# Two modulation parts as matmuls of 32 columns between the product terms, weights split on one engine, wider parts and earlier token norms

## The chip, the cores and the metric

The kernel runs on one core of a Trainium2 chip. TensorE is called PE here, VectorE DVE, ScalarE ACT, GpSimd POOL, SyncE SP (it issues DMAs). The metric is the time of one execution in device microseconds (us); the lower the better. PE's clock has two levels here, 1.2 and 2.4 GHz, and the profile gives the granted share of the upper one.

## The reference, cut to what matters

One transformer block for 1024 tokens of width 1024, all in float32. The change lies in the first part only: the modulation vectors, the first norm, and the combined input projection (1024 x 1280) whose columns are Fourier channels (512), queries (512), keys (128) and values (128).

```
ada = silu(c) @ w_ada + b_ada                  # c: 1 x 1024, w_ada: 1024 x 6144
sh1, sc1, g1, sh2, sc2, g2 = split(ada, 6)     # six parts of 1024
h = rmsnorm(x, norm_mix_g) * (1 + sc1) + sh1   # 1024 tokens x 1024
uqkv = h @ w_in                                # 1024 x 1280
...                                            # Fourier mix, windowed attention, w_out
x = x + g1 * mixed
h = rmsnorm(x, norm_ffn_g) * (1 + sc2) + sh2
...                                            # expert-choice MoE, 16 experts
return x + g2 * moe
```

## The kernel before, in words

A float32 product is made of three matmuls: each operand is split in a rounded high part and the rest (`split`, lines 76 to 78: ACT writes hi, another engine lo = src - hi), and hi x hi, lo x hi and hi x lo are summed in PSUM. `wh`/`wl` are the halves of a weight chunk of `w_in` (128 rows x 1280), `hh`/`hl` those of the transposed, normed and modulated tokens `hf`.

Three phases: modulation and input projection, up to about 183 us; Fourier mix, attention, output projection and router, up to 459 us; then the 16 experts.

In the first phase the tokens stand in 8 tiles (t) of 128, the width in 8 chunks (k) of 128. **The pair**: tiles 0 and 1 are multiplied together, chunk by chunk, while the 8 chunks of `w_in` and the columns of parts 1 (sc1) and 0 (sh1) of `w_ada` still arrive. For each k or pair of ks, `load_mod` brings columns of both parts (128 x 8 x 256, or halves of 128 x 4 x 512), `mod_mac` multiplies them on DVE with silu(c) and sums over j (L111 for the first, L113 for the rest), `mod_sum` sums over the partitions with matmuls against `ones` (L209), and `mod_cols` makes the columns G1c and sh1c from that (L216 to L218). `chunk` transposes (L226), applies G1c and sh1c on ACT (L233, hf) and splits into hh (ACT, L77) and hl (POOL, L78). `take` splits the weights: wh on ACT (L349), then `low_w` makes wl (L277), the first `WLO[k]` columns on POOL and the others on DVE. `project` (L332) issues a unit: for each of hh x wh, hl x wh, hh x wl and each tile, three matmuls of 512, 512 and 256 columns into three PSUM accumulators (names pu, pu, pv, or px for the second tile of the pair).

**Tiles 2 to 7** follow, each in two chunks of four units (m = 0 to 11, the steps of `seq`): m = 0, 1 are tile 2, m = 2, 3 tile 3, and so on. The last kv accumulator of each tile stands in one PSUM buffer (pv, one buffer), which `finish` empties on ACT (L338 un, L340 kk, L341 vf) and DVE (L339). Beside them run, in steps after each unit (`bg_tick`): `qknorm` for each tile done (squares on ACT, sums on DVE L245, then on POOL a power L248, and the products L252, L254 and L257 into kd; two transposes on PE, L264, and the split of their result into khi and klo), and `ada_row` for the four other parts of `w_ada`, in 8 rows of 512 columns (DVE macs L111 and L113, one matmul with `ones` on PE, L142, an add on DVE, L143, and a store). The norm of the next tile but one's tokens is `norm_x`: ACT squares with a sum (L152), DVE, POOL's power (xr, L155), ACT's scaling of the tokens in place (L186).

Up to the last product of the pair the order on each engine is the order of the code (`in_order`). Behind that a scheduler sets the order of each engine when the program is built. Each engine runs its instructions strictly in that order, so that an instruction that waits holds up all behind it.

Of the kernel before, what the change touches and what calls it, by code (L numbers as in the profile page):

```python
# [11 lines left out]
F32 = mybir.dt.float32  # L12
# [9 lines left out]
NT = 8  # L22
# [10 lines left out]
SCRATCH = 4096  # L33
WLO = (0, 768, 768, 1280, 768, 1280, 768, 768)
SB, PB, WB, YB = 9, 2, 4, 3
# [8 lines left out]
def block_kernel(ctx: ExitStack, tc: tile.TileContext, t_in, out):  # L44
# [35 lines left out]
    def raw(shape):  # L80
        return raw1.tile(shape, F32, name="raw", tag="raw")
# [3 lines left out]
    c_t = cst.tile([128, 8], F32, name="c_t")  # L85
    c_act = cst.tile([128, 8], F32, name="c_act")
    cols = cst.tile([128, 4, 8], F32, name="cols")
# [42 lines left out]

    def ada_row(acc, br, px, part, cc):
        col = part * 1024 + cc * 512
        for jh in range(2):
            u = raw([128, 4, 512])
            SP.dma_start(u, w_ada_v[:, jh * 4:jh * 4 + 4, col:col + 512])
            for j in (0, 2):
                mac(acc, u[:, j:j + 2], 2, jh * 4 + j)
                yield
        SP.dma_start(br, b_ada[:, col:col + 512])
        yield  # L140
        p = px()
        PE.matmul(p[0:1], ones[:, 0:1], acc, start=True, stop=True)  # L142
        DVE.tensor_tensor(br, p[0:1], br, op=OP.add)  # L143
        SP.dma_start(md[part - 2:part - 1, cc * 512:cc * 512 + 512], br)

# [65 lines left out]

# [8 lines left out]
    def chunk(ts, kc0, nk):  # L220
# [59 lines left out]
    mods, maccs, msums = {}, {}, {}  # L280
    load_mod(0)
# [40 lines left out]
    def ada_all():  # L322
        for part in (2, 4, 3, 5):
            for cc in range(2):
                yield from ada_row(racc, br[0:1], px, part, cc)

    def project(ts, kc, hs_, o):
        for l, r in ((0, w_h), (1, w_h), (0, w_l)):
            for s_ in range(len(ts)):
                lhs = hs_[l][:, o + s_ * 128:o + s_ * 128 + 128]  # L330
                for acc, c0, c1 in zip(accs[s_], (0, 512, 1024), (512, 1024, 1280)):
                    PE.matmul(acc[:, :c1 - c0], lhs, r[kc][:, c0:c1], start=(kc == 0 and l == 0 and r is w_h),  # L332
                              stop=(kc == 7 and r is w_l))

    def finish(s_, t):
        au, aq, ak = accs[s_]
        kk = ust.tile([128, 128], F32, name="kk", bufs=2)
        ACT.activation(u_n[t], au, AF.Copy)  # L338
        DVE.tensor_copy(qn[t], aq)  # L339
        ACT.activation(kk, ak[:, :128], AF.Copy)  # L340
        ACT.activation(vf[:, t, :], ak[:, 128:256], AF.Copy)  # L341
        bg.append(qknorm(t, kk))

    pair = (0, 1)
    accs = [[pu(), pu(), (pv, px)[s_]()] for s_ in pair]

    def take(k):
        r = wraw.pop(k)
        ACT.activation(w_h[k], r, AF.Copy)  # L349
        if WLO[k] == 1280:  # L350
            low_w(k, r)
            h = chunk(pair, k, 1)
        else:
            h = chunk(pair, k, 1)
            low_w(k, r)
# [23 lines left out]
    take(2)
    column(4)  # L380
    take(3)
    column(5)
    project(pair, 2, hs.pop(2), 0)
    scales(4, 5)
    take(4)
    load_x(2)
    column(6)
    project(pair, 3, hs.pop(3), 0)
    take(5)
    column(7)  # L390
    load_x(3)
    project(pair, 4, hs.pop(4), 0)
    project(pair, 5, hs.pop(5), 0)
    scales(6, 7)
    take(6)
# [38 lines left out]
    for m, (t, kc0) in enumerate(seq):  # L434
        hs_ = nxt
        if m == len(seq) - 1:
# [4 lines left out]
            for n, wid in ((4, 512), (2, 256), (1, 128), (1, 128)):  # L441
                basis(n, wid)
        if kc0 == 0:
            if t + 2 < NT:
                load_x(t + 2)
            if t + 1 < NT:
                norm_x(t + 1)
            accs = [[pu(), pu(), pv()]]
        if m + 1 < len(seq):
            nxt = chunk((seq[m + 1][0],), seq[m + 1][1], 4)  # L450
        for a in range(4):
            project((t,), kc0 + a, hs_, a * 128)
            if m == 0 and a == 1:
                DVE.scalar_tensor_tensor(gg, qg, HD ** -0.5, kg, op0=OP.mult, op1=OP.mult)
# [891 lines left out]
```

## Time and profile before

| | us |
|---|---|
| runs of the kernel before | 1076.07, 1079.47, 1079.58 (median 1079.47) |
| the profiled execution | 1078.71, its span 1076.90, mean granted PE clock 0.949 |
| start to the first product of the pair | 0 to 16.12 |
| the pair, k = 0 to 7 | 16.12 to 70.50 |
| m = 0, 1 | 70.50 to 87.72 |
| m = 2 | 87.72 to 105.91 |
| m = 3 to 9 | 105.91 to 168.97 |
| m = 10, 11 | 168.97 to 183.20 |
| Fourier mix, attention, output projection, router | 183.20 to 459.00 |
| 16 experts | 459.00 to 1076.90 |

The bounds of the stages are the starts of matmuls of line L332 in the timeline of PE (70.50 is the first matmul of m = 0, and so on). Each row of a timeline is a run of like instructions: start, time from the first start to the last end, engine, line, operation, output and inputs, partitions x elements, count, and in square brackets the idle time ahead of it and who ended it. A float32 matmul leaves two records. A matmul's record ends later than the next may start, so that what one costs is read from start to start.

### The profile page before, as it was taken

How to read it: one execution, taken by the hardware profiler on the slowest of the kernel's cores; microseconds unless marked ns; L12 is line 12 of the kernel's file. 1: busy time of each engine (PE TensorE's matmuls, PEld its weight loads, DVE VectorE, ACT ScalarE, POOL GpSimd, SP SyncE). 2: the span in 40 equal slices, each digit the busy share in tenths (PEclk: the TensorE clock that was granted, in tenths of full speed). 3: DMA queues.
4: the chain of work that ended last, by engine and by line, in shares of the span. 5: the costliest groups of instructions: out<-in, count | busy, mean ns of one | idle time of the engine just before them, and what ended most of it. 6: DMA issues, size and time to landing. Idle time of an engine off the chain costs nothing.

```text
span 1076.9 us, 13229 instructions
## 1 busy us (share of the span) xinstructions
PE 969.0 (90%) x4681; PEld 756.4 (70%) x4681; DVE 845.9 (79%) x1223; ACT 636.9 (59%) x846; POOL 540.3 (50%) x345
## 2 busy tenths in 40 slices
PE   4797999979999996496769999999999999999996
PEld 3675767747777675374658777877787778777885
DVE  6845884687666959689688898889888988898894
ACT  3353434576455442264437777777777777777782
POOL 2646465132433334355472875587558755772203
PEclk9798999979999999598889999999999999999998
DMA  9765674262312136895689999999999999999922
GB/s 318 246 210 212 220 266 150 82 195 61 111 70 89 65 132 215 326 321 192 229 260 339 410 372 374 369 411 370 373 369 411 371 371 371 411 371 358 376 110 40
DMA packets 95499, 283.97 MB, mean 264 GB/s; under 512 B 7892, under 2 KB 25480, under 8 KB 95304
## 3 DMA queue, kind: packets, MB, share of 16 engines
q1 hardware_dynamic: 90824, 266.34, 66.7%
q0 software_dynamic: 4608, 16.78, 6.1%
q8 instruction: 37, 0.61, 0.2%
q14 instruction: 30, 0.25, 0.1%
HBM read 263.79 MB, written 21.40 MB: 265 GB/s over the span
## 4 chain that ended last, share of the span: by engine, by line
PE 64%; DVE 15%; issue 6%; ACT 4%; DMA 2%; POOL 2%; POOLq 0%; DVEq 0%; ACTq 0%; SPq 0%
PE pa L72 13%; PE pa L73 13%; PE pa L74 13%; PE pu L332 4%; PE pt L1192 2%; ACT wh L77 2%; PE pt L640 2%; PE yp L653 2%; DVE sc L805 2%; DVE wl L78 2%; PE pj L74 2%; PE pj L72 2%; PE pj L73 2%; DVE sc L806 2%; DVE ws L113 2%
## 5 line engine op out<-in xcount | busy, mean ns | idle before, releaser
L78 DVE TENSOR_TENSOR wl<-raw,wh 128x2048 fp32r<-128x2048 f32 (+1 forms) x183 | 418.1, 2309 | 63.5 <-ACT wh L77 62.6
L77 ACT ACTIVATE wh<-raw 128x2048 fp32r<-128x2048 f32 (+2 forms) x209 | 367.8, 1780 | 85.0 <-PE pa L73 81.3
L1165 POOL TENSOR_SCALAR oneh<-tri_f,pos 128x128 bf16<-128x128 f32 x102 | 189.5, 1871 | 4.1 <-PE pa L1047 3.3
L73 PE MATMUL pa<-wh,t1l 128*128 128x512 f32 x384 | 151.8, 395 | 7.8 <-DVE t1l L78 7.8
L72 PE MATMUL pa<-wh,t0h 128*128 128x512 f32 x384 | 155.8, 406 | 0.0
L73 PE MATMUL pa<-wh,t0l 128*128 128x512 f32 x384 | 153.4, 400 | 0.0
L72 PE MATMUL pa<-wh,t1h 128*128 128x512 f32 x384 | 153.1, 399 | 0.0
L74 PE MATMUL pa<-wl,t0h 128*128 128x512 f32 x384 | 152.6, 397 | 0.0
L74 PE MATMUL pa<-wl,t1h 128*128 128x512 f32 x384 | 151.3, 394 | 0.0
L1207 POOL TENSOR_TENSOR ys<-ys,g_r 128x512 f32<-128x512 f32 x30 | 53.5, 1803 | 124.7 <-ACT ys L1206 124.7
L73 PEld LDWEIGHTS pa<-wh,t1l 128*128 128x128 f32 x384 | 72.6, 189 | 24.0 <-DVE t1l L78 8.3
L74 PEld LDWEIGHTS pa<-wl,t0h 128*128 128x128 f32 x384 | 73.6, 192 | 17.0
L72 PEld LDWEIGHTS pa<-wh,t0h 128*128 128x128 f32 x384 | 73.6, 192 | 16.2 <-ACT t0h L77 0.2
L73 PEld LDWEIGHTS pa<-wh,t0l 128*128 128x128 f32 x384 | 73.6, 192 | 16.1 <-DVE t0l L78 0.4
L74 PEld LDWEIGHTS pa<-wl,t1h 128*128 128x128 f32 x384 | 72.6, 189 | 17.0 <-DVE wl L78 0.4
L72 PEld LDWEIGHTS pa<-wh,t1h 128*128 128x128 f32 x384 | 72.4, 189 | 15.9
L1182 POOL DMA_INDIRECT xe<-h2d,idx x16 | 16.9, 1055 | 115.7 <-DVE gt L1179 110.7
L78 POOL TENSOR_TENSOR wl<-raw,wh 128x1024 fp32r<-128x1024 f32 (+1 forms) x26 | 56.7, 2208 | 22.3 <-ACT wh L77 22.2
L78 POOL TENSOR_TENSOR hl<-hf,hh 128x512 fp32r<-128x512 f32 (+1 forms) x20 | 25.5, 1274 | 62.9 <-ACT hh L77 43.6
L1210 POOL DMA_INDIRECT out_dram<-ys,idx x16 | 50.9, 3183 | 10.6 <-DVE ys L1209 6.4
L611 DVE CUSTOM_DVE_ANT_0 sb<-lg,bias,sink 128x384 f32<-128x384 f32 (+1 forms) x64 | 35.0, 579 | 26.7 <-PE lg L609 15.7
L233 ACT ACTIVATE hf<-pt,sh1c,G1c 128x128 f32<-128x128 f32 (+1 forms) x56 | 22.6, 479 | 53.3 <-PE pt L226 36.2
(310 smaller groups left out, 1809.5 us busy)
## 6 DMA issues: line engine op xcount, KB each, us to landing
raw<-in_w_gate_dram SPq DMA_DIRECT2D x64, 1024.0 KB
raw<-in_w_up_dram SPq DMA_DIRECT2D x64, 1024.0 KB
raw<-in_w_down_dram SPq DMA_DIRECT2D x63, 1024.0 KB
raw<-in_w_ada_dram SPq DMA_DIRECT2D x16, 1024.0 KB
raw<-in_w_ada_dram SPq DMA_DIRECT2D x16, 512.0 KB
xt<-in_x_dram SPq DMA_DIRECT2D x8, 512.0 KB
raw<-in_w_out_dram SPq DMA_DIRECT2D x4, 1024.0 KB
raw<-in_x_dram SPq DMA_DIRECT2D x8, 512.0 KB
```

The lines of the kernel that those rows point to most:

```text
L72: PE.matmul(o, lh, rh, start=start, stop=False)
L73: PE.matmul(o, ll, rh, start=False, stop=False)
L74: return PE.matmul(o, lh, rl, start=False, stop=stop)
L77: ACT.activation(hi, src, AF.Copy)
L78: return (eng or DVE).tensor_tensor(lo, src, hi.bitcast(F32), op=OP.subtract)
L113: DVE.scalar_tensor_tensor(acc, u[:, j, :], w, acc, op0=OP.mult, op1=OP.add)
L233: ACT.activation(hf[:, a * w:a * w + w], tp[:, a * w:a * w + w], AF.Identity, scale=G1c[:, kc:kc + 1], bias=sh1c[:, kc:kc + 1])
L332: PE.matmul(acc[:, :c1 - c0], lhs, r[kc][:, c0:c1], start=(kc == 0 and l == 0 and r is w_h), stop=(kc == 7 and r is w_l))
L611: DVE.tensor_tensor_reduce(sb[:, :wid], lg[:, :wid], bias[:, kv * 4 + i, j0:j0 + wid], 1.0, sk[:, i:i + 1], op0=OP.add, op1=OP.max, accum_ ...
L1165: (POOL if t < shared else DVE).tensor_scalar(oneh[:, t, :], slots, pos[:, t, e:e + 1], None, op0=OP.is_equal)
L1207: POOL.tensor_tensor(ys[:, cs_], ys[:, cs_], g2_r[:, cs_], op=OP.mult)
L1210: POOL.indirect_dma_start(out=out2, out_offset=bass.IndirectOffsetOnAxis(ap=idx[:, :1], axis=0), in_=ys, in_offset=None, compute_op=OP.add)
```

## The change

- `c_act` becomes 128 x 8 x 32, zero but for its first column. `part_row` multiplies it (32 columns as stationary operand) with the raw columns of `w_ada`, on PE; term j goes to the PSUM partitions 32g to 32g + 31 with g = j mod 4, in one bank (px). This takes the place of `mod_mac` on DVE. `mod_sum` copies that bank to SBUF on ACT and sums it with `ones`.
- `terms` is `project` as a generator; the part rows stand in PE's order between its second term (hl x wh) and its third (hh x wl).
- wl and hl are made on DVE alone, 1280 and up to 512 wide. POOL has neither.
- In the pair `pair_chunk` (hf, hh, hl) stands ahead of `weights` (wh, wl). Four loads of modulation columns and three of weights are issued at once.
- The pair's two key and value accumulators share one bank (pv). Tiles 2 to 7 alternate between px and pv. The transposes of kd go to pt from the start.
- The four other parts of `w_ada` are made 1024 wide: raws of 128 x 2 x 1024, two to three fetched ahead, 8 macs for a part, two matmuls (32 columns, two column groups) and one add of 64 x 512.
- Token tiles are loaded three ahead and normed two ahead; tiles 2 and 3 are both normed ahead of the pair's last two products. `finish` does the query copy, kk and vf ahead of un.

The core of the diff:

```diff
-WLO = (0, 768, 768, 1280, 768, 1280, 768, 768)
+    def part_row(p, g, j, u, start, stop):
+        PE.matmul(p[32 * g:32 * g + 32, :u.shape[-1]], c_act[:, j, :], u, start=start, stop=stop)
...
     def mod_mac(h):
-        ks, j, n = halves[h]
-        if j == 0:
-            maccs[ks] = qn[4 + (0, 1, 2, 0, 3, 0, 0)[ks[0]]][:, :len(ks) * 256]
-        mac(maccs[ks], mods.pop(h), n, j)
+        ks, j0, n = halves[h]
+        if j0 == 0:
+            msums[ks] = px()
+        u = mods.pop(h)
+        for j in range(n):
+            part_row(msums[ks], (j0 + j) % 4, j0 + j, u[:, j], j0 + j < 4, j0 + j >= 4)
     def mod_sum(*ks):
-        acc = maccs.pop(ks)
-        mp = pt()
+        mp = msums[ks]
+        acc = qn[4 + (0, 1, 2, 0, 3, 0, 0)[ks[0]]][:, :len(ks) * 256]
+        ACT.activation(acc, mp[:, :len(ks) * 256], AF.Copy)
...
-        split(hi[:, :n], lo[:, :n], hf[:, :n], POOL)
+        split(hi[:, :n], lo[:, :n], hf[:, :n])
...
-    px_ = [px]
+    px_ = [pt]
...
     def low_w(kc, r):
-        c = WLO[kc]
-        for eng, c0, c1 in ((POOL, 0, c), (DVE, c, 1280)):
-            if c0 < c1:
-                eng.tensor_tensor(w_l[kc][:, c0:c1], r[:, c0:c1], w_h[kc][:, c0:c1].bitcast(F32), op=OP.subtract)
+        after["w"] = DVE.tensor_tensor(w_l[kc], r, w_h[kc].bitcast(F32), op=OP.subtract)
...
+    def ada_parts(acc, br, parts):
...
+        fetch()
+        fetch()
+        for part in parts:
+            for q in range(4):
+                fetch()
+                u = us.pop(0)
+                for j in range(2):
+                    yield
+                    mac(acc, u[:, j:j + 1], 1, 2 * q + j)
...
+            p = pt()
+            for g in range(2):
+                PE.matmul(p[32 * g:32 * g + 32], ones[:, 0:32], acc[:, 512 * g:512 * g + 512], start=True, stop=True)
+            yield
+            DVE.tensor_tensor(br, p[:64], br, op=OP.add)
...
+    def pair_products(k, n):
+        p = terms(pair, k, hs.pop(k), 0)
+        next(p)
+        next(p)
+        if n < 8:
+            column(n)
+            column(n + 1)
+        drain(p)
+        if n < 8:
+            scales(n, n + 1)
+        p = terms(pair, k + 1, hs.pop(k + 1), 0)
+        next(p)
+        if n < 8:
+            pair_chunk(n)
+            weights(n)
+        next(p)
+        if n < 8:
+            pair_chunk(n + 1)
+        drain(p)
+        if n < 8:
+            weights(n + 1)
...
-                load_x(t + 2)
-            if t + 1 < NT:
-                norm_x(t + 1)
-            accs = [[pu(), pu(), pv()]]
+                load_x(t + 3)
+            if t + 2 < NT:
+                norm_x(t + 2)
+            accs = [[pu(), pu(), (px, pv)[t % 2]()]]
```

In ACT's order around k = 1 and k = 2 (wh with its number is the high half of one weight chunk; hh is that of the tokens' chunk), before:

```order
L349 ACTIVATE wh_154<-ws 128x1280
L233 ACTIVATE hf<-pt,sh1c,G1c 128x256
L77 ACTIVATE hh<-hf 128x256
L349 ACTIVATE wh_156<-u_hi 128x1280
L233 ACTIVATE hf<-pt,sh1c,G1c 128x256
L77 ACTIVATE hh<-hf 128x256
```

and after:

```order
L241 ACTIVATE qn_117<-px 128x256
L266 ACTIVATE hf<-pt,sh1c,G1c 128x256
L76 ACTIVATE hh<-hf 128x256
L384 ACTIVATE wh_159<-ws 128x1280
L241 ACTIVATE qn_118<-px 128x512
L266 ACTIVATE hf<-pt,sh1c,G1c 128x256
L76 ACTIVATE hh<-hf 128x256
L384 ACTIVATE wh_161<-u_hi 128x1280
```

The copy of the part rows came in, and wh of a chunk moved from ahead of that chunk's hh to behind it.

In PE's order around the start of m = 2 (the first rows are its first unit or units), before:

```order
L332 MATMUL pu<-wh_152,hh 128x512 x2
L332 MATMUL pv<-wh_152,hh 128x256
L332 MATMUL pu<-wh_152,hl 128x512 x2
L332 MATMUL pv<-wh_152,hl 128x256
L332 MATMUL pu<-wl_153,hh 128x512 x2
L332 MATMUL pv<-wl_153,hh 128x256
L332 MATMUL pu<-wh_154,hh 128x512 x2
L332 MATMUL pv<-wh_154,hh 128x256
L332 MATMUL pu<-wh_154,hl 128x512 x2
L264 MATMUL px<-ident,kd 128x128 x2
L332 MATMUL pv<-wh_154,hl 128x256
```

and after:

```order
L259 MATMUL pt<-ident,xt 128x128 x4
L362 MATMUL pu<-wh_157,hh 128x512 x2
L362 MATMUL pv<-wh_157,hh 128x256
L362 MATMUL pu<-wh_157,hl 128x512 x2
L362 MATMUL pv<-wh_157,hl 128x256
L362 MATMUL pu<-wl_158,hh 128x512 x2
L362 MATMUL pv<-wl_158,hh 128x256
L297 MATMUL pt<-ident,kd 128x128 x4
```

Both pairs of transposes of kd (tiles 0 and 1) now stand together behind the first unit, on the two buffers of pt; before they stood in the second and the third unit, on px. The second pair takes the buffer of pt that the chunk of m = 3 (the L259 ahead of the unit) fills and that ACT's hf of that chunk (L266) empties.

In ACT's order over the same place, after (L217 is the scaling of a token tile that `norm_x` ends with, here of tile 5; the last hf is that of m = 3's chunk):

```order
L276 ACTIVATE ws<-qn_109 128x512
L266 ACTIVATE hf<-pt,sh1c,G1c 128x128 x4
L183 ACTIVATE junk,xs<-xt 128x1024
L76 ACTIVATE hh<-hf 128x512
L217 ACTIVATE xt<-xt,xr 128x1024
L375 ACTIVATE un_122<-pu 128x512
L373 ACTIVATE kk<-px 128x128
L374 ACTIVATE vf<-px 128x128
L275 ACTIVATE ws<-kk 128x128
L266 ACTIVATE hf<-pt,sh1c,G1c 128x128 x4
```

The scaling stands ahead of tile 2's `finish` and of the hf of m = 3, as its counterpart L186 (there of tile 4) did before.

And in POOL's order, after, up to that tile's xr (the last row):

```order
L186 TENSOR_TENSOR xr<-xs,mhalf 128x1 x3
L281 TENSOR_TENSOR qr<-qs,mhalf 128x10
L285 TENSOR_TENSOR qn_108<-qn_108,qr 128x512
L287 TENSOR_TENSOR kk<-kk,qr 128x128
L290 TENSOR_TENSOR kd<-kk,gg 128x2x64 x2
L281 TENSOR_TENSOR qr<-qs,mhalf 128x10
L285 TENSOR_TENSOR qn_109<-qn_109,qr 128x512
L287 TENSOR_TENSOR kk<-kk,qr 128x128
L290 TENSOR_TENSOR kd<-kk,gg 128x2x64 x2
L186 TENSOR_TENSOR xr<-xs,mhalf 128x1
```

The two splits hl that stood ahead of and behind this chain are gone; the chain of both tiles still stands ahead of xr.

## Rows read from the trace of the kernel before

**Rows 1.** The page's chain of the work that ended last, by engine, as shares of the span.

```profile
PE 64%; DVE 15%; issue 6%; ACT 4%; DMA 2%; POOL 2%; POOLq 0%; DVEq 0%; ACTq 0%; SPq 0%
```

**Rows 2.** The windows of the stages: start and end, length, busy time (and count) of PE, PE's weight loads, DVE, ACT and POOL, PE's granted clock, share of the DMA engines, GB/s.

```profile
16.12:70.50 54.38, 43.49 (x195) 35.10 (x195) 39.16 (x54) 20.78 (x34) 26.48 (x18) 0.87 0.71 239
70.50:87.72 17.22, 17.22 (x86) 12.84 (x85) 11.44 (x19) 8.57 (x22) 12.02 (x9) 1.00 0.94 334
87.72:105.91 18.19, 11.91 (x49) 8.80 (x48) 8.90 (x14) 5.36 (x13) 11.11 (x12) 0.81 0.52 177
105.91:168.97 63.06, 60.56 (x303) 45.44 (x302) 48.70 (x71) 27.91 (x65) 31.44 (x26) 1.00 0.66 234
168.97:183.20 14.23, 14.23 (x76) 12.00 (x75) 5.37 (x9) 3.47 (x12) 10.82 (x11) 1.00 0.37 115
183.20:459.00 275.80, 240.99 (x1289) 175.28 (x1288) 198.71 (x616) 139.40 (x373) 94.75 (x88) 0.91 0.40 136
459.00:1076.90 617.90, 578.40 (x2690) 465.46 (x2690) 526.47 (x430) 425.39 (x323) 351.14 (x175) 0.97 0.89 329
```

**Rows 3.** The timeline of PE in the pair: the first matmuls of the products k = 0, 1, 2, 3, 4 and 6, and the sum of the modulation columns 4 and 5.

```profile
16.12 1.22 PE L332 MATMUL pu<-wh,hh 128*128 128x512 f32 x2 [1.16 <-ACT hh L77]
...
24.68 0.73 PE L332 MATMUL pu<-wh,hh 128*128 128x512 f32 x2 [1.54 <-ACT hh L77]
...
32.41 0.74 PE L332 MATMUL pu<-wh,hh 128*128 128x512 f32 x2 [0.63 <-ACT hh L77]
...
42.58 1.83 PE L209 MATMUL pt<-ones,qn 128*128 128x2 f32 x8 [5.24 <-DVE qn L113]
...
44.59 1.20 PE L332 MATMUL pu<-wh,hh 128*128 128x512 f32 x2
...
50.44 0.70 PE L332 MATMUL pu<-wh,hh 128*128 128x512 f32 x2
...
60.12 0.73 PE L332 MATMUL pu<-wh,hh 128*128 128x512 f32 x2 [0.63 <-ACT hh L77]
```

**Rows 4.** Windows of two stretches behind a long idle time of PE (columns as in rows 2).

```profile
44.59:50.44 5.85, 5.85 (x23) 4.89 (x21) 5.67 (x9) 2.14 (x3) 4.27 (x3) 0.60 0.00 0
94.71:99.80 5.09, 5.09 (x16) 4.21 (x17) 0.82 (x1) 2.58 (x7) 1.30 (x1) 0.50 0.79 294
```

**Rows 5.** The timeline of PE at one of the ada rows (L142, one float32 matmul of 512 columns, two records) with the transpose behind it, and in the attention, where two float32 matmuls of 256 columns go to two halves of the array, 64 columns each (L653, four records), with the transposes behind them.

```profile
150.01 1.02 PE L142 MATMUL px<-ws,ones 128*1 128x512 f32 x2
150.96 0.33 PE L226 MATMUL pt<-ident,xt 128*128 128x128 f32 x1
...
394.69 0.65 PE L653 MATMUL yp<-pT,vf 128*64 128x256 f32 x4
395.27 0.66 PE L752 MATMUL pt<-ident,raw 128*128 128x128 f32 x4
```

**Rows 6.** The same view of PE for a stretch of 20 ns at one of those pairs: the records that began in it.

```profile
391.72 0.44 PE L653 MATMUL yp<-pT,vf 128*64 128x256 f32 x2 [0.48 <-DVE ss L724]
```

**Rows 7.** The timeline of ACT: one weight split in the pair, between two splits of the tokens.

```profile
24.53 1.28 ACT L349 ACTIVATE wh<-u_hi 128x1280 fp32r<-128x1280 f32 x1
```

**Rows 8.** The timeline of DVE: a weight chunk's low half done whole, the macs of the modulation columns 4 and 5 in the pair, and a mac of 1024 columns in the second phase.

```profile
14.67 1.48 DVE L277 TENSOR_TENSOR wl<-ws,wh 128x1280 fp32r<-128x1280 f32 x1
...
32.26 10.17 DVE L113 SCALAR_TENSOR_TENSOR qn<-raw,c_act,qn 128x512 f32<-128x512 f32 x7
...
241.76 1.21 DVE L872 SCALAR_TENSOR_TENSOR G_r<-G_r,raw 128x1024 f32<-128x1024 f32 x1
```

**Rows 9.** The timeline of PE in m = 0 and 1: the bias table's matmul and one ada row.

```profile
74.19 1.02 PE L456 MATMUL pt<-ws,rb 32*8 32x512 f32 x2
...
84.58 1.02 PE L142 MATMUL px<-ws,ones 128*1 128x512 f32 x2
```

**Rows 10.** The timeline of PE at the start of m = 2.

```profile
87.72 0.71 PE L332 MATMUL pu<-wh,hh 128*128 128x512 f32 x2
94.71 0.58 PE L332 MATMUL pv<-wh,hh 128*128 128x256 f32 x1 [6.28 <-ACT vf L341]
```

**Rows 11.** The timeline of ACT at that place: the scaling of tile 4's tokens, and the hf of the chunk behind it.

```profile
92.70 1.15 ACT L186 ACTIVATE xt<-xt,xr 128x1024 f32<-128x1024 f32 x1 [10.17 <-POOL xr L155]
...
94.74 1.51 ACT L233 ACTIVATE hf<-pt,sh1c,G1c 128x128 f32<-128x128 f32 x4
```

**Rows 12.** The timeline of POOL ahead of that: the first step of tile 0's key and query norms, the split hl that follows tile 1's last step, and tile 4's xr.

```profile
77.27 2.45 POOL L248 TENSOR_TENSOR qr<-qs,mhalf 128x10 f32<-128x10 f32 x1 [1.18 <-DVE qs L246]
...
89.97 1.73 POOL L78 TENSOR_TENSOR hl<-hf,hh 128x512 fp32r<-128x512 f32 x1
91.66 1.00 POOL L155 TENSOR_TENSOR xr<-xs,mhalf 128x1 f32<-128x1 f32 x1
```

**Rows 13.** The groups of instructions by line and shape in m = 3 to 9, of PE and of DVE: busy time, mean ns of one, idle time ahead of them and what ended it.

```profile
L142 PE MATMUL px<-ws,ones 128*1 128x512 f32 x12 | 6.1, 590 | 2.2 <-DVE ws L113 2.1
...
L113 DVE SCALAR_TENSOR_TENSOR ws<-raw,c_act,ws 128x512 f32<-128x512 f32 x42 | 36.5, 868 | 0.9
```

**Rows 14.** The waits of PE from 16 to 70.5 us: engine, tile and line, what it waited for, us in total, times, longest.

```profile
PE pt L209 <- DVE qn L113: 5.2, 1, 5.2
PE pu L332 <- ACT hh L77: 3.9, 4, 1.5
...
PE pu L332 <- POOL wl L277: 0.8, 1, 0.8
```

More of the change, by code (lines that the diff above doesn't have):

```diff
@@ L85, in block_kernel @@
     c_t = cst.tile([128, 8], F32, name="c_t")
-    c_act = cst.tile([128, 8], F32, name="c_act")
+    c_act = cst.tile([128, 8, 32], F32, name="c_act")
     cols = cst.tile([128, 4, 8], F32, name="cols")
@@ L97, in block_kernel @@
     SP.dma_start(c_t, t_in["c"].rearrange("b (p j) -> (b p) j", j=8))
-    ACT.activation(c_act, c_t, AF.Silu)
+    POOL.memset(c_act, 0.0)
+    ACT.activation(c_act[:, :, 0], c_t, AF.Silu)
     POOL.memset(ones, 1.0)
@@ L129, in drain, with fetch, store @@
             pass
[L131 to L144, printed above, removed]
+    def ada_parts(acc, br, parts):
+        todo = [(part, q) for part in parts for q in range(4)]
+        us, rows_ = [], []
+        def fetch():
+            if todo:
+                part, q = todo.pop(0)
+                us.append(raw([128, 2, 1024]))
+                SP.dma_start(us[-1], w_ada_v[:, 2 * q:2 * q + 2, part * 1024:part * 1024 + 1024])
+        def store():
+            if rows_:
+                part = rows_.pop()
+                for g in range(2):
+                    SP.dma_start(md[part - 2:part - 1, g * 512:g * 512 + 512], br[32 * g:32 * g + 1])
+        fetch()
[7 more added lines that the diff above has]
+                    mac(acc, u[:, j:j + 1], 1, 2 * q + j)
+                if q == 0:
+                    store()
+                if q == 1:
+                    for g in range(2):
+                        c0 = part * 1024 + 512 * g
+                        SP.dma_start(br[32 * g:32 * g + 1], b_ada[:, c0:c0 + 512])
+            yield
+            p = pt()
+            for g in range(2):
+                PE.matmul(p[32 * g:32 * g + 32], ones[:, 0:32], acc[:, 512 * g:512 * g + 512], start=True, stop=True)
+            yield
+            DVE.tensor_tensor(br, p[:64], br, op=OP.add)
+            rows_.append(part)
+        store()
     w_ada_v = w_ada.rearrange("(p j) c -> p j c", j=8)
@@ L292, in block_kernel @@
     load_mod(2)
+    load_mod(3)
+    wraw[2] = load_w(2)
     rb = p1.tile([32, 8], F32, name="rb")
@@ L322, in ada_all, with terms @@
     def ada_all():
[L323 to L327, printed above, removed]
+        yield from ada_parts(racc, br, (2, 4, 3, 5))
+    def terms(ts, kc, hs_, o):
         for l, r in ((0, w_h), (1, w_h), (0, w_l)):
@@ L331, in project @@
                 for acc, c0, c1 in zip(accs[s_], (0, 512, 1024), (512, 1024, 1280)):
-                    PE.matmul(acc[:, :c1 - c0], lhs, r[kc][:, c0:c1], start=(kc == 0 and l == 0 and r is w_h),
-                              stop=(kc == 7 and r is w_l))
+                    first = kc == 0 and l == 0 and r is w_h and not (s_ and c0 == 1024)
+                    PE.matmul(acc[:, :c1 - c0], lhs, r[kc][:, c0:c1], start=first, stop=(kc == 7 and r is w_l),
+                              skip_group_check=c0 == 1024)
+            yield
+    def project(ts, kc, hs_, o):
+        drain(terms(ts, kc, hs_, o))
     def finish(s_, t):
@@ L341, in finish, with weights @@
         ACT.activation(vf[:, t, :], ak[:, 128:256], AF.Copy)
+        ACT.activation(u_n[t], au, AF.Copy)
         bg.append(qknorm(t, kk))
     pair = (0, 1)
-    accs = [[pu(), pu(), (pv, px)[s_]()] for s_ in pair]
-    def take(k):
+    both_kv = pv()
+    accs = [[pu(), pu(), both_kv[:, 256 * s_:256 * s_ + 256]] for s_ in pair]
+    def weights(k):
         r = wraw.pop(k)
         ACT.activation(w_h[k], r, AF.Copy)
[L350 to L355, printed above, removed]
+        low_w(k, r)
         if k + 3 < 8:
             wraw[k + 3] = load_w(k + 3)
-        hs[k] = h
     def column(h):
         mod_mac(h)
-        if h + 3 < 8:
-            load_mod(h + 3)
+        if h + 4 < 8:
+            load_mod(h + 4)
     def scales(*ks):
@@ L367, in scales, with pair_chunk @@
         mod_cols(*ks)
-    hs = {}
-    take(0)
-    column(1)
-    project(pair, 0, hs.pop(0), 0)
+    def pair_chunk(k):
+        hs[k] = chunk(pair, k, 1)
+    def pair_products(k, n):
[19 more added lines that the diff above has]
+            weights(n + 1)
+    hs = {}
+    weights(0)
+    load_mod(4)
+    pair_chunk(0)
+    p = terms(pair, 0, hs.pop(0), 0)
+    next(p)
+    next(p)
+    column(1)
+    drain(p)
+    scales(1)
+    pair_chunk(1)
+    weights(1)
+    p = terms(pair, 1, hs.pop(1), 0)
+    next(p)
+    next(p)
     column(2)
-    scales(1)
-    take(1)
     column(3)
-    project(pair, 1, hs.pop(1), 0)
+    drain(p)
     scales(2, 3)
[L379 to L385, printed above, removed]
+    pair_chunk(2)
+    weights(2)
+    pair_chunk(3)
+    weights(3)
+    pair_products(2, 4)
     load_x(2)
[L387 to L390, printed above, removed]
     load_x(3)
[L392 to L395, printed above, removed]
+    pair_products(4, 6)
     norm_x(2)
-    take(7)
+    norm_x(3)
     project(pair, 6, hs.pop(6), 0)
@@ L402, in block_kernel @@
     ws = [stage(), stage()]
-    sq, racc = ws[0][:, :640], ws[0][:, 640:1152]
-    br = ws[1][:, :512]
+    sq, br = ws[0][:, :640], ws[0][:64, 640:1152]
+    racc = ws[1][:, :1024]
+    POOL.memset(br, 0.0)
     for s_ in pair:
@@ L453, in block_kernel @@
             if m == 0 and a == 1:
-                DVE.scalar_tensor_tensor(gg, qg, HD ** -0.5, kg, op0=OP.mult, op1=OP.mult)
+                with tc.issue_after(after["w"].ins):
+                    DVE.scalar_tensor_tensor(gg, qg, HD ** -0.5, kg, op0=OP.mult, op1=OP.mult)
                 p = pt()
@@ L891, in block_kernel @@
     ydone, x2s, x2Ts, xts, ylive = {}, {}, {}, {}, [0]
-    after = {}
     fr, qks, ready, sp = {}, {}, [], [None]
```

14 lines of the change are left out of this document (6 added, 8 removed).

## The prediction

> **What bounds the kernel now.** I read the chain of the work that ended last first: PE holds 64% of it [rows 1]. Then the windows by stage [rows 2]: the change touches only what ends at 183.20 us, and there PE is either busy or waited for in every stretch. In m = 0, 1 and in m = 10, 11 it is busy all the time (17.22 of 17.22, 14.23 of 14.23), in m = 3 to 9 for 60.56 of 63.06. So what counts is PE's own work, and its waits, which the page's waits put in two places. In the pair (54.38 us, 43.49 of them busy) it waits 5.2 us for DVE's macs, four times for hh, 3.9 us in all, and 0.8 for POOL's share of wl [rows 14]. In m = 2 it waits 6.28 us for ACT's vf [rows 10]. Both long waits cost twice: behind the first the granted clock is 0.60 over 5.85 us, behind the second 0.50 (the lower level, 1.2 GHz) over 5.09 [rows 4]. The second and third phases, 275.80 and 617.90 us, begin with work that needs the last tile's projection, and their code is unchanged; I let them shift as a block, by what 183.20 shifts.
>
> A unit of the projection takes 14.23 / 8 = 1.78 us at the full clock, the transposes with it [rows 2], a product of the pair (two tiles) 3.5, two of its three terms 2.4, or 4.7 at the lower level.
>
> **The cost of a part row.** No row of before has a stationary operand of 32 columns in four column groups. A float32 matmul of 512 columns alone takes 0.95 us from start to next start (150.01 to 150.96) [rows 5]. Two in two column groups do run together: both began within 20 ns [rows 6], and the two of 256 columns took 0.58 (394.69 to 395.27) [rows 5] where one alone would take half of 0.95, 0.48. So the bounds for four of 512 are 0.95 (all at once) and 3.8 (one after another). I take 0.95, nearest to the row with two groups, whose surplus over one is only 0.10. Eight rows of 512 then are 1.9 us, the 256 wide set 1.0, or 1.6 at the lower level.
>
> The Trainium skill speaks against full packing: "TensorE: Matmul & The Clock Gate", section "Measured speedup vs the span model", gives 2.38 times for three column tiles of 32 and N = 512, 3.07 times for four row tiles. By that four would take 4 x 0.95 / 3.07 = 1.24 us, an estimate, and the sum below would be 2 us worse; no run here shows it yet.
>
> **The pair, stretch by stretch** (the times of before are the differences of their starts [rows 3]). The first product starts at 16.2 (16.12): the part rows of set 0 replace 8 macs, but ACT's squares of the tokens still hold its copy.
> - k = 0 to 1, before 8.56: plus 1.6 for part rows at the lower level, plus 1.27 because wh of k = 1 now stands behind hh in ACT's order (a split takes 1.28 [rows 7]) and PE needs both, minus 0.6, since the third term then runs at the full level. 10.85, so 27.05.
> - k = 1 to 2, before 7.73: plus 1.9 and 1.27 likewise. 10.9, so 37.95.
> - k = 2 to 3, before 12.18, with the wait for DVE of 5.24. That wait goes, since DVE has no macs, and POOL's 0.8 goes too. What remains is two terms 3.75 (I let half of it fall in the lower level), part rows 1.9, third term 1.2, sum 0.8. 7.65, so 45.6. The copy on ACT, as long as un's, lies beside the third term.
> - k = 3 to 4, before 5.85 at 0.60 of the clock: without the idle time ahead of it 4.25, so 49.85.
> - k = 4 to 6, before 9.68: plus 1.9 part rows and 0.8 for the sum and its transposes, minus 1.9 for the wait for the chunk, which now lies beside k = 5. 10.5, so 60.35.
> - k = 6 to m = 0, before 10.38: plus 1.0 as the bias table's matmul (1.02, 74.19 [rows 9]) now stands ahead of m = 0; the two token norms ahead of the products hold the transposes of tile 2 for about as long as before. 11.15, so 71.5.
>
> The pair: +1.0 us. The gain from the wait is spent on part rows (7.3 in all) and on wh. DVE's wl (1.48 for a chunk alone [rows 8]) lies beside the first two terms; if it should not, 0.3 to 1 us at each of the seven.
>
> **m = 0, 1.** The bias matmul (1.0, moved) and an ada row (0.95, 84.58 [rows 9]) go, with their gaps 2.5 us. 17.22 to 14.75, so m = 2 starts at 86.2 (87.72).
>
> **m = 2: the wait changes its place.** Before, PE waited for pv, emptied by ACT behind the scaling at 92.70, which waited 10.17 us for POOL's xr [rows 11]; that stood behind the norms of tiles 0 and 1, from 77.27 to 89.97, and a split of 1.73 [rows 12]. With px and pv in turn this wait goes. But both pairs of transposes of kd now stand behind the first unit of m = 2, and the second pair needs the buffer that hf of m = 3 frees; that hf stands on ACT behind a scaling (tile 5) that needs an xr behind the same chain on POOL. The sums of tile 0 come later: on DVE ahead of them stand the bias add and five macs of 1024 (1.21 each [rows 8]); I get 80.05 for the chain's start. 80.05 + 12.7 (as 77.27 to 89.97) = 92.75, xr 1.0 = 93.75, from the scaling to the end of hf 3.6 (92.70 to 96.25 [rows 11]) = 97.4. PE reaches the place at 88.1 and waits 9.2 us, then loses some 2.5 at the lower level, as in rows 4. Behind it are 3 units, the transposes of kd and an ada sum: m = 3 starts at 107.0 (105.91). 20.8 for 18.19, +2.6. Queued behind the waiting transposes is all of PE's work; ACT's khi and DVE's klo of tiles 0 and 1 come late, and nobody needs them before the attention.
>
> **m = 3 to 9.** Seven chunks of 4 units at 7.37 are 51.6. Before, six ada rows (12 records, 6.1 busy), 2.1 us of waits for their macs [rows 13], the kd transposes and small gaps make the rest of 63.06. After, three pairs of ada sums, each pair in two column groups at 1.0, and 1.4 of kd transposes: 55.9, so -7.1. DVE bears it: 42 macs of 868 ns [rows 13] become about half as many of 1.21 plus contention, and the splits hl come to it, 0.7 each; POOL, which split weights beside DVE's macs in the pair, where they took 10.17 / 7 = 1.45 each [rows 8], loses its splits. m = 10, 11 stay at 14.2.
>
> **The sum.** +1.0 - 2.5 + 2.6 - 7.1 = -6.0. I add 1.5 for small waits for DVE (in m = 1 to 8 it is busy some nine tenths of PE's time, and hl now queues behind macs of 1.21): -4.5. Against the profiled execution that is 1078.71 - 4.5 = 1074.2; the median stands 0.76 above it, so I say 1074.5. Unknown sizes: the wait in m = 2 (7 to 12 us, so +-2.5), the clock in the pair (+-2), DVE (0 to 4): the likeliest case's own range is 1069.5 to 1079.
>
> **The rivals.**
> - Part rows packed less well. If four groups give only what two give in rows 5, 0.95 / 0.58 = 1.64 of 2, that is 3.3 of 4: 1.15 for 0.95, +0.2 for each of 7 sets; if they go in pairs, +0.95 for each, 6.5 us: 1076 to 1081. For it: no row shows four. Against: the 20 ns.
> - **Slower: the part rows go one after another.** Each half of a set then costs 3.8 in place of 0.95, six halves +17, the narrow set +3, on PE's path since the third term waits behind them: +20, partly made up by waits that shrink, so 1088 to 1094. It decides from 1.6 us for a half: there -4.5 is used up. For it: all four write one bank. Against: the two groups of rows 6 do so too.
> - The wait in m = 2 does not come: POOL's chain without its splits, and the ada loads that no longer hold DVE, let xr come before 90. 1065 to 1070. For it: two splits leave POOL. Against: the chain's start hangs on DVE, with longer macs.
> - DVE becomes the bound of tiles 2 to 6: if the macs of 1024 cost twice 868 ns, a tile has 8 of 1.74 plus 4.3 of other work, 18.2 us for a PE time of 16; -7.1 falls to about 0, 1081.
>
> **How the numbers follow.** As forecast 0.55, packed less 0.20, one after another 0.08, no wait in m = 2 0.08, DVE the bound 0.09. A measurement of this kernel tells about 0.5% (5.4 us) from no change. Faster by more: half of the first case (0.28), a fifth of the second and the whole fourth, 0.40. Slower by more: the third, a tail of the second and the last, 0.15. Within: 0.45. The range leaves out most of the third case and the end of the fourth: 1067 to 1084.
>
> **What would show it.** In the profile after: the four L117 of a half start together and the half takes about 1 us; PE's third product starts without a wait for DVE; wh, not hh, ends the waits at k = 1 and 2; an idle time of 7 to 12 us ahead of the second pair of L297 at 88 us, ended by POOL's kd or ACT's hf, with 0.5 of the clock behind it; m = 3 to 9 at 56 us with little waiting for DVE. I am wrong if a half takes over 1.6 us, if that wait is missing, or if hl on DVE ends waits of PE in every chunk.

## The result, and the profile after

The changed kernel took 1072.54 us (median of 5 runs, 1069.07 to 1073.78), before 1079.47: the ratio is 0.9932, with a 95% interval of 0.9910 to 0.9955. Its profiled execution took 1073.78, with a span of 1071.9 and a mean granted clock of 0.952.

The stages, from the same starts of matmuls (of L362 now):

| stage | before | forecast | after |
|---|---|---|---|
| first product of the pair | 16.12 | 16.2 | 16.93 |
| the pair | 54.38 | 55.3 | 54.57 |
| m = 0, 1 | 17.22 | 14.75 | 15.05 |
| m = 2 | 18.19 | 20.8 | 18.95 |
| m = 3 to 9 | 63.06 | 55.9 | 56.52 |
| m = 10, 11 | 14.23 | 14.2 | 14.38 |

The windows of after, with the columns of [rows 2]:

```profile
16.93:71.50 54.57, 47.91 (x261) 34.16 (x261) 16.80 (x34) 23.71 (x39) 1.63 (x3) 0.94 0.88 300
71.50:86.55 15.05, 15.05 (x82) 12.77 (x81) 14.15 (x18) 9.69 (x24) 6.96 (x5) 1.00 0.83 286
86.55:105.50 18.95, 11.48 (x51) 8.38 (x50) 6.67 (x11) 5.15 (x13) 11.84 (x13) 0.73 0.36 139
105.50:162.02 56.52, 56.52 (x303) 45.64 (x302) 40.80 (x48) 26.21 (x62) 23.65 (x17) 1.00 0.64 233
```

In the pair DVE's busy time fell from 39.16 to 16.80 and POOL's from 26.48 to 1.63, and PE's rose from 43.49 to 47.91: the work moved, and the stage took the same time. From m = 3 to 9 PE is busy all the time, and most of the gain lies there (6.54 us; m = 0, 1 gives 2.17, and the other stages lose a little). At the first matmul of the second phase after is ahead by 184.36 - 177.41 = 6.95 us. The profiled execution gives 2 us of it back further on: its second phase took 276.66 us up to the first product of the experts, before 273.72, and what follows took 1 us less. In the kernels below, with the same code there, the second phase took 272.6 to 274.6; why it was longer in this execution isn't shown. So the two profiled executions are 4.93 apart, the medians 6.93.

The timeline of PE in the pair of after (L117 are the part rows, two records each; L259 the transposes of tile 2), against [rows 3]:

```profile
21.49 1.60 PE L117 MATMUL px<-raw,c_act 128*32 128x256 f32 x16
...
27.64 0.74 PE L362 MATMUL pu<-wh,hh 128*128 128x512 f32 x2 [2.57 <-ACT wh L384]
...
30.18 1.92 PE L117 MATMUL px<-raw,c_act 128*32 128x512 f32 x16
...
37.12 1.22 PE L362 MATMUL pu<-wh,hh 128*128 128x512 f32 x2 [2.36 <-ACT wh L384]
...
41.68 2.60 PE L117 MATMUL px<-raw,c_act 128*32 128x512 f32 x16
...
46.28 0.72 PE L362 MATMUL pu<-wh,hh 128*128 128x512 f32 x2
...
66.03 0.66 PE L259 MATMUL pt<-ident,xt 128*128 128x128 f32 x4 [1.73 <-ACT xt L217]
```

A set of eight rows of 512 takes 1.92 at the full clock; at 30.18 three of its records began within 20 ns and a fourth within 120 ns, so the four groups do run together. The wait of 5.24 for DVE is gone, and wh, no longer hh, ends the waits at k = 1 and 2. Behind the second of them the products run at the lower level (the record of 1.22 for two matmuls, 0.72 at the upper one).

And at m = 2 of after, on PE, with the granted clock behind this wait and behind that at k = 2 in two windows, against [rows 10] and [rows 4]:

```profile
88.39 0.38 PE L297 MATMUL pt<-ident,kd 128*128 128x128 f32 x2
96.24 0.66 PE L297 MATMUL pt<-ident,kd 128*128 128x128 f32 x2 [7.47 <-ACT hf L266]
```

```profile
96.24:101.75 5.51, 5.51 (x16) 3.39 (x16) 2.16 (x5) 1.44 (x4) 2.71 (x2) 0.56 0.00 0
37.12:44.21 7.09, 7.09 (x28) 3.96 (x28) 3.30 (x3) 1.98 (x3) 0.00 (x0) 0.58 0.89 283
```

On ACT, where the scaling of tile 5 waits for POOL's xr and the hf of m = 3 stands behind it, and on POOL, against [rows 11, 12]:

```profile
92.53 1.15 ACT L217 ACTIVATE xt<-xt,xr 128x1024 f32<-128x1024 f32 x1 [9.11 <-POOL xr L186]
...
94.58 1.51 ACT L266 ACTIVATE hf<-pt,sh1c,G1c 128x128 f32<-128x128 f32 x4
```

```profile
80.95 1.97 POOL L281 TENSOR_TENSOR qr<-qs,mhalf 128x10 f32<-128x10 f32 x1 [4.51 <-DVE qs L279]
...
91.12 0.87 POOL L290 TENSOR_TENSOR kd<-kk,gg 128x128 f32<-128x128 f32 x2
91.94 0.56 POOL L186 TENSOR_TENSOR xr<-xs,mhalf 128x1 f32<-128x1 f32 x1
```

The wait changed its place as forecast, from pv to the second pair of transposes of kd, through the same scaling and the same chain on POOL.

### The profile page after: what moved, and what is told of

Its sections match the earlier page's. It is cut to its first block, busy times and chain, and to the rows that moved or that the text cites. A ratio compares the mean times of both kernels' runs of the same rounds, so it can differ in the third digit from the quotient of the medians.

```text
span 1071.9 us, 13300 instructions
## 1 busy us (share of the span) xinstructions
PE 966.7 (90%) x4761; PEld 754.1 (70%) x4761; DVE 813.2 (76%) x1169; ACT 639.3 (60%) x851; POOL 503.8 (47%) x320
## 4 chain that ended last, share of the span: by engine, by line
PE 70%; DVE 14%; issue 6%; ACT 5%; DMA 2%; POOL 2%; SPq 0%; POOLq 0%; ACTq 0%; DVEq 0%
PE pa L71 13%; PE pa L72 13%; PE pa L73 13%; PE pu L362 7%; PE pt L1249 2%; ACT wh L76 2%; PE yp L711 2%; DVE sc L863 2%; PE pt L698 2%; DVE wl L77 2%; PE pj L71 2%; PE pj L72 2%; PE pj L73 2%; DVE sc L864 2%; PE pt L821 1%
## 5 line engine op out<-in xcount | busy, mean ns | idle before, releaser
L71 PEld LDWEIGHTS pa<-wh,t0h 128*128 128x128 f32 x384 | 73.3, 191 | 16.2 <-ACT t0h L76 0.2
L76 ACT ACTIVATE t0h<-pt 128x512 fp32r<-128x512 f32 x32 | 17.9, 597 | 55.2 <-PE pt L1249 55.2
L775 POOL TENSOR_TENSOR raw<-raw 128x512 f32<-128x512 f32 x12 | 15.6, 1301 | 73.7 <-DVE raw L774 54.6
```

The lines of the kernel that those rows point to most:

```text
L71: PE.matmul(o, lh, rh, start=start, stop=False)
L76: ACT.activation(hi, src, AF.Copy)
```

## The experiments

Each is an edit of the changed kernel; ratios are to the kernel before, on the same chip. "The last product" is the end of L362's last record, 176.54 in after.

**Part rows in one column group, in two, in four.** With one group:

```diff
-            part_row(msums[ks], (j0 + j) % 4, j0 + j, u[:, j], j0 + j < 4, j0 + j >= 4)
+            part_row(msums[ks], 0, j0 + j, u[:, j], j0 + j == 0, j0 + j == 7)
...
-        ACT.activation(acc, mp[:, :len(ks) * 256], AF.Copy)
+        ACT.activation(acc[:32], mp[:32, :len(ks) * 256], AF.Copy)
...
```

Expected: 

> The changed kernel with all part rows of the two modulation parts in one column group (PSUM partitions 0 to 31) in place of four. Theory (the four groups run together): a half of 4 rows takes 3.8 us in place of 0.96, the six halves +17, the narrow set +2 to +4, all on PE's path: m = 0 starts at 90 to 94 in place of 71.5, time 1090 to 1095, slower than the kernel before by 1.0 to 1.5%. Rival (the groups gain little, and the part rows lie beside waits for weights): under +4 us, so about 1073 to 1077.

1087.34 us, ratio 1.0100 (1.0076 to 1.0123). With two groups (g = j mod 2, 64 rows copied and summed), expected: 

> The changed kernel with the part rows in two column groups in place of four. Theory (time goes with the number of rows in a group): a set of eight rows of 512 takes 3.6 to 3.9 us (1.92 with four groups, 7.05 with one), m = 0 starts at 77 to 79, time 1077 to 1080. Rival (two groups do as well as four, the limit lies elsewhere): a set takes under 2.5 us.

One run: 1076.39 us, m = 0 at 76.80, both just under the theory's range. The timelines of PE, one group at the sets of columns 4 and 5 and of 6 and 7, and then two groups at the set of columns 4 and 5:

```profile
49.96 7.17 PE L117 MATMUL px<-raw,c_act 128*32 128x512 f32 x16
...
65.86 7.05 PE L117 MATMUL px<-raw,c_act 128*32 128x512 f32 x16
```

```profile
43.63 3.63 PE L117 MATMUL px<-raw,c_act 128*32 128x512 f32 x16
```

A set takes 7.05 us with one group (at 65.86, and at 33.77 likewise), 3.63 with two, 1.92 with four, so four give 7.05 / 1.92 = 3.67 times. m = 0 starts at 90.09, 76.80 and 71.50. Both theories of the groups hold in what a set takes, and the rivals fall; the time with one group is 2.7 us under its range, though m = 0 starts where it should, and the time with two groups rests on a single run.

**The modulation parts back on DVE**, all else as changed:

```diff
-            part_row(msums[ks], (j0 + j) % 4, j0 + j, u[:, j], j0 + j < 4, j0 + j >= 4)
+        mac(msums[ks], mods.pop(h), n, j0)
...
-        ACT.activation(acc, mp[:, :len(ks) * 256], AF.Copy)
```

Expected: 

> The changed kernel with the two modulation parts back on DVE (8 macs a set, no part rows and no copy on ACT), all else as changed. Theory (the part rows spend on PE about what they save in waits, and the lower clock behind the waits decides): PE loses 7.3 us of part rows and gains three waits for DVE's macs of 2 to 5 us with the lower clock behind them, m = 0 starts at 71 to 77, time 1072 to 1078. Rival (the part rows are the change's main gain): m = 0 starts after 79, time 1080 or more. Other rival (they are a loss): m = 0 starts before 70, time under 1071.

1079.40 us, ratio 1.0006 (0.9987 to 1.0026). PE's timeline at the three sums of columns that come late:

```profile
33.23 1.02 PE L240 MATMUL px<-ones,qn 128*128 128x2 f32 x8 [2.43 <-DVE qn L113]
...
46.63 1.84 PE L240 MATMUL px<-ones,qn 128*128 128x2 f32 x8 [3.43 <-DVE qn L113]
...
63.10 1.84 PE L240 MATMUL px<-ones,qn 128*128 128x2 f32 x8 [5.15 <-DVE qn L113]
```

The waits are as expected, 11.0 us in all, but their price is more: the clock granted from 16 to 74 us is 0.79, and m = 0 starts at 81.2, past the theory's range. My theory falls and the first rival holds, but for the time, 0.6 under its bound: without the part rows nothing is left of this change's gain, once DVE has wl and hl as well. That doesn't make them the only source of it: the wide ada sums, undone alone below, take it all away too.

**The weight split ahead of hh again at k = 1 and 2:**

```diff
+    weights(1)
     pair_chunk(1)
-    weights(1)
...
+    weights(2)
     pair_chunk(2)
-    weights(2)
```

Expected: 

> The changed kernel with the weight split wh ahead of hf and hh on ACT at k = 1 and k = 2, as in the kernel before. Theory (wh behind hh costs its own length twice): the waits ahead of those two products fall from 2.57 and 2.36 us to 1.3 and 1.1, m = 0 starts at about 69, time 1070. Rival (something later in the pair, the token norms ahead of chunk 6 or arriving weights, sets the pair's end): the waits fall, but m = 0 starts at 71 to 71.5 as before and the time stays at 1072.5.

1066.24 us, ratio 0.9884 (0.9860 to 0.9909). PE's timeline at k = 1 and 2, and the windows of the pair and of the product k = 2:

```profile
26.55 0.73 PE L362 MATMUL pu<-wh,hh 128*128 128x512 f32 x2 [1.41 <-ACT hh L76]
...
34.85 0.74 PE L362 MATMUL pu<-wh,hh 128*128 128x512 f32 x2 [1.20 <-ACT hh L76]
```

```profile
17.36:66.51 49.15, 44.88 (x261) 32.42 (x261) 16.55 (x34) 23.75 (x39) 1.62 (x3) 1.00 0.94 329
34.85:41.30 6.45, 6.45 (x42) 4.28 (x43) 2.50 (x4) 2.58 (x4) 0.00 (x0) 1.00 1.08 369
```

The two waits shrink by 2.3 us, as expected, but the pair by 54.57 - 49.15 = 5.4: the clock is granted whole at k = 2 (1.00, where after has 0.58), and from that product's start to the next takes 6.45 us in place of 9.16. The theory holds in its direction, and gained more than it said: m = 0 starts at 66.51, not at 69, and the time is 3.8 us under its 1070.

That the shorter waits brought the whole clock isn't shown. Two other kernels of this section speak against the length of the wait alone. At k = 2, the first below with wh first too (its time is 1061.97), the second with the part rows in two groups:

```profile
34.35 1.03 PE L360 MATMUL pu<-wh,hh 128*128 128x512 f32 x2 [1.20 <-ACT hh L76]
```

```profile
41.10 0.73 PE L362 MATMUL pu<-wh,hh 128*128 128x512 f32 x2 [2.27 <-ACT wh L384]
```

Behind the wait of 1.20 the granted clock is 0.79 and the next product starts 8.02 us later; behind the one of 2.27 it is 1.00. The pair took 49.15, 49.29 and 50.13 us in the three kernels with wh first, 53.61 to 54.82 in after and the four kernels with the same code in the pair, so wh's place is worth 3.5 to 5.7 us there, of which 2.3 are the waits themselves.

**The norms of tiles 5 to 7 one chunk later**, so that the scaling no longer stands ahead of the hf of m = 3:

```diff
-            if t + 2 < NT:
+            if t == 2:
                 norm_x(t + 2)
...
+        if kc0 == 4 and 2 < t < NT - 2:
+            norm_x(t + 2)
         if m + 1 < len(seq):
             nxt = chunk((seq[m + 1][0],), seq[m + 1][1], 4)
```

Expected: 

> The changed kernel with the norms of tiles 5, 6 and 7 issued one chunk later, so that the scaling of tile 5 no longer stands on ACT ahead of the hf of m = 3. Theory (ACT's hf behind the scaling is the last of two causes of the 7.5 us wait in m = 2, POOL's kd of tile 1 the next): the wait falls to 3 to 4 us and is ended by POOL kd; time 1066 to 1069. Rival (POOL's chain alone sets it, the scaling only coincides): the wait stays above 6.5 us, time 1072.

1075.06 us, ratio 0.9970 (0.9954 to 0.9987). With the transposes of kd of tiles 0 and 1 four steps later as well (`for _ in range(8 if t < 2 else 4): yield`), expected: 

> The kernel of the norms one chunk later, and the transposes of kd of tiles 0 and 1 four steps later too (second unit of m = 3). Theory (the wait is only one of order): no wait of over 1 us in m = 2, the clock stays at its upper level, m = 3 starts near 95 in place of 105.5, time 1061 to 1064. Rival (DVE and POOL set the pace of tiles 2 and 3): PE waits for hh, hl or the macs of the ada sum in m = 2 to 4 instead, and under 5 us are gained, 1068 or more.

1075.11 us, ratio 0.9977 (0.9958 to 0.9996). PE's timeline with the norms later:

```profile
91.52 0.44 PE L297 MATMUL pt<-ident,kd 128*128 128x128 f32 x2 [3.63 <-POOL kd L290]
...
127.26 1.05 PE L171 MATMUL pt<-ws,ones 128*32 128x512 f32 x4 [2.71 <-DVE ws L113]
...
146.01 1.29 PE L171 MATMUL pt<-ws,ones 128*32 128x512 f32 x4 [2.51 <-DVE ws L113]
```

The wait in m = 2 falls to 3.63 us and POOL's kd ends it, just as the theory says, and m = 3 starts at 100.08 for 105.50. But the last product ends at 178.42, later than 176.54. What came in its place stands ahead of the wait at 127.26, on ACT and on DVE of the same kernel:

```profile
120.55 1.15 ACT L217 ACTIVATE xt<-xt,xr 128x1024 f32<-128x1024 f32 x1 [7.48 <-POOL xr L186]
121.61 1.49 ACT L266 ACTIVATE hf<-pt,sh1c,G1c 128x128 f32<-128x128 f32 x4
```

```profile
123.79 0.69 DVE L77 TENSOR_TENSOR hl<-hf,hh 128x512 fp32r<-128x512 f32 x1 [4.52 <-ACT hh L76]
124.40 1.28 DVE L113 SCALAR_TENSOR_TENSOR ws<-raw,c_act,ws 128x1024 f32<-128x1024 f32 x1
```

The scaling of the next tile stands ahead of an hf here too, and waits 7.48 us for POOL; DVE waits for that chunk's hh, with two macs behind it, and PE for the macs. In the second kernel m = 2 runs without a wait, m = 3 starts at 94.79, and there the transposes of kd wait 5.02 us for the hf of m = 4, which stands behind the same scaling. The theory of one wait out of order fell, and the rival of the second kernel is right in its numbers (waits for macs and hf elsewhere, over 1068). What it names as the cause, the pace of DVE and POOL, falls with the kernels below: the same scaling made three different waits.

**The norms behind the chunk's hf.** So I put the later norms behind `nxt = chunk(...)` instead of ahead of it, with wh first and the later transposes of kd. With the ada sums one step later besides (one more `yield` ahead of `p = pt()` in `ada_parts`), expected: 

> The changed kernel with four edits: wh ahead of hh at k = 1 and 2; the norms of tiles 5 to 7 one chunk later and behind that chunk's hf; the transposes of kd of tiles 0 and 1 four steps later; the ada sums one step later. Theory (in the two kernels that removed the wait in m = 2 the gain went to waits for the ada macs, which stand on DVE behind an hl that waits for hh; with the sums a step later these waits go): no wait over 1 us from m = 2 to 11, the last product ends at 160 to 162, time 1054 to 1058. Rival (DVE has too little time for the macs of a part in a tile whatever the order): waits for DVE's macs of 4 us or more in m = 3 to 9, the last product at 167 or later, time 1062 or more.

Without that step: 

> The same without the step more ahead of the ada sums. Theory (the order of the sums against the macs is what costs): waits for DVE's macs of 3 to 6 us in m = 3 to 9, time 1060 to 1063. Rival (the place of the norms alone was at fault): within 1 us of the kernel with the later sums.

1059.16 us, ratio 0.9831 (0.9807 to 0.9855), and 1061.97, ratio 0.9857 (0.9837 to 0.9878). PE's timeline of the first from m = 2 on, where it waits:

```profile
98.58 0.41 PE L296 MATMUL pt<-ident,kd 128*128 128x128 f32 x2 [2.77 <-DVE klo L77]
...
119.96 1.05 PE L172 MATMUL pt<-ws,ones 128*32 128x512 f32 x4 [0.23 <-DVE ws L113]
```

The last product ends at 164.71 and 167.01. From the start of m = 0 to there it took 105.0 us in after, 104.7 with wh first alone, 107.8 and 108.8 in the two kernels with the norms merely later, and 98.5 and 99.4 here. So wh's place changes next to nothing behind the pair, and it is the norms behind the hf that bring the gain. The first kernel misses its theory's numbers a little (one wait of 2.77 us is left, the last product ends 2.7 us and the time is 1.2 us past the range), but its rival, 4 us or more of waits for macs, is out. In the second there is no wait for the macs at all, where I expected 3 to 6 us: its time lies in the theory's range, but not for the theory's reason. The rival's reason holds better, the place of the norms, though the two medians are 2.8 us apart, not within 1. Of the 2.3 us between the two profiles 1.4 lie ahead of m = 0, where their code is the same, so the step is worth about 0.9 here; the medians don't settle more, as the runs of the two overlap (1056.72 to 1061.15, 1060.07 to 1063.28). The first is the best kernel of this study.

**hl of tiles 2 to 7 back on POOL** (`split(..., POOL if len(ts) == 1 else None)`). Expected: 

> The changed kernel with the splits hl of tiles 2 to 7 back on POOL (the pair's stay on DVE). Theory (taking hl from POOL shortened the chain ahead of xr and freed PE of waits for it): the wait in m = 2 grows from 7.5 us to 9 or 10 and PE waits for hl or kd in some chunks of m = 3 to 9, time 1075 to 1079. Rival (hl's engine is indifferent, the gain of m = 3 to 9 is that of the ada sums alone): 1071.5 to 1073.5.

1073.32 us, ratio 0.9960 (0.9946 to 0.9975). PE's timeline in m = 2:

```profile
89.57 0.73 PE L362 MATMUL pu<-wh,hl 128*128 128x512 f32 x2 [2.67 <-POOL hl L77]
...
95.09 0.66 PE L297 MATMUL pt<-ident,kd 128*128 128x128 f32 x2 [3.87 <-ACT hf L266]
```

The waits of the theory are there (4.9 us for hl, in four places), but the one in m = 2 splits in two without growing, and the time is the rival's.

**The other parts in rows of 512 again**, as in the kernel before, on pt. Expected: 

> The changed kernel with the four other parts of w_ada in 8 rows of 512 as before (one column, one matmul each, on pt). Theory (the ada sums in pairs and the macs of 1024 are the gain of m = 3 to 9): 8 sums of 0.95 in place of 4 of 1.0, and 2 us of waits for macs come back, m = 3 to 9 takes 60 to 62 in place of 56.5, time 1076 to 1079. Rival (the gain comes from hl and the two kv banks): m = 3 to 9 stays under 58, time 1072 to 1074.

1078.68 us, ratio 1.0007 (0.9995 to 1.0019). The window of m = 3 to 9:

```profile
102.94:169.14 66.20, 62.98 (x304) 46.72 (x302) 48.16 (x77) 25.86 (x62) 18.66 (x17) 0.93 0.57 193
```

66.20 us for 56.52, more than expected: without the ada sums and macs of 1024 that stage has no gain left. The theory's time holds, its waits don't: of the 9.7 us 3.2 are waits, but only 0.5 of them for macs, the others for hf, hl and hh. Here m = 2 took 16.49 for 18.95, and up to the end of the last product the kernel is 183.64 - 176.54 = 7.1 behind. The whole execution of this profile has a clock of 0.911, so its stages are a little long (m = 10, 11 take 14.46).

Not undone alone were px and pv in turn, the earlier norms and the earlier loads; what each is worth stays open.

## Why the prediction was right

**What was right.** The time (1074.5 forecast, 1072.54 measured) lies in the likeliest case's own range, and the stages that were to change moved the way that was forecast. A half of a set of part rows was put at 0.95 us, between 0.95 and 3.8: it takes 0.96. The Trainium skill's figures that I weighed against it ("TensorE: Matmul & The Clock Gate", section "Measured speedup vs the span model": 2.38 times for three column tiles, 3.07 for four row tiles) were too low a guide for four column groups: 3.67 times here. The row of two groups that began within 20 ns was the better guide. The rival of rows one after another had its price nearly right, 1088 to 1094: one group gave 1087.34. m = 0 was to start at 71.5, and does. The wait in m = 2 moved to the second pair of kd transposes, with the cause that the order showed. From m = 3 to 9 the rows of 512 undone gave back the gain.

**What was off, by term.** The pair's sum hid two errors of about 1.5 us that cancel in this execution: the lower clock came at k = 2, not at k = 1 (9.48 us from k = 1 to 2 for 10.9, then 9.16 to k = 3 for 7.65, with the part rows at 2.60). Where the lower clock falls changes from one profile to the next, though: three others with the same code in the pair took 10.96 to 11.01 and then 7.85 to 8.01, near to the forecast. The first product starts 0.8 us later than before, not 0.1: ACT's squares of the tokens begin at 9.25 instead of 8.58 as the tokens arrive later; in the other kernels the product starts at 16.3 to 18.3, so I leave the cause open. The stage furthest off is m = 2, 18.95 for 20.8. Its wait was put at 9.2 and is 7.47: POOL's chain began 0.9 us later than I put it, but took 11.0 us, not 12.7, xr took 0.56, not 1.0, and PE came to the place 0.7 us later. (The chain's last three steps took 2.3 us where before took 3.7; DVE was idle beside them, and had macs before. That this is the reason isn't shown.) The margin of 1.5 us for DVE was used by nothing: PE has no wait for DVE from m = 1 to 9 in after. Without it the sum of the terms was -6.0, and the measured one up to the second phase is -6.95.

Three numbers of the working don't follow from its own: 10.38 plus 1.0 for the last stretch of the pair is 11.4, not 11.15 (it took 10.83); the 7.37 for four units stands in no row and is more than four times the 1.78 (m = 1 took 7.44); and 1074.2 plus 0.76 is 1075.0, not 1074.5. They are small; where the second comes from isn't told, though it is near what was measured.

**What the prediction did not see.** I wrote that the gain from the wait for DVE "is spent on part rows ... and on wh". That holds against the kernel before, and says little about the parts: undone alone, the part rows cost 6.9 us of the median (1079.40 for 1072.54) and wh's place had cost 6.3 (1066.24); in ratios to the kernel before, each on its own chip, 0.74% and 0.48%. So the change is a sum of larger gains and a loss, and the forecast had only its balance right. I priced wh at its length twice, 2.5 us; the waits are that long, and in after the lower clock stood behind the second. And I treated the wait in m = 2 as one that could be absent or present; removing it at its place gained nothing, because the scaling that waits for POOL stood ahead of an hf wherever the norm was put, until it was put behind it.

## What to carry to other kernels

When a wait is removed at one place and the time doesn't follow, look for the instruction that waits in order on another engine, here a scaling of a tile that nobody needs yet: ask what is queued behind it, and move it behind that, not only later. A vector as stationary operand, padded to 32 columns and spread over four column groups, made a matrix-vector product on PE cheap enough (1.92 us for eight rows of 512) to stand between other matmuls. A wait of PE is to be priced with the clock that may stand behind it, and over several executions: here 2.3 us of waits gone went with 5.4 between two of them, and with 3.5 to 5.7 over all kernels that share the code.

## What the runs showed of the hardware

The time of the part rows falls almost as the number of column groups rises: a set of eight float32 rows of 512 takes 7.05, 3.63 and 1.92 us in one, two and four groups. The length of a wait alone does not tell the clock behind it: in after the granted clock was 1.00 behind a wait of 2.57 us at k = 1 and 0.58 behind one of 2.36 at k = 2; with two groups it was 1.00 behind one of 2.27; with wh first, at the same wait of 1.20, it was 1.00 in two kernels and 0.79 in a third. And the first product's two terms took 4.56 us (16.93 to 21.49), almost twice their time at k = 4, while the profile grants 1.00 there: the durations show the lower level where that column doesn't.
